# Splitting the probabilities and v of layer 0 into hi and lo parts, with two v tiles in flight

## The chip, the cores and the metric

The kernel runs on one core of one Trainium2 chip. The metric is the device time of one execution in microseconds (us), taken several times; the median counts. One of the executions is recorded by the hardware profiler, and all trace times below count from the start of that span. TensorE's matmuls are called PE, its weight loads PEld, VectorE DVE, ScalarE ACT, GpSimd POOL and the DMA queue's engine SP.

## What is computed

Two layers of a generator over 512 latent and 256 context tokens, width 1024. Only the mixer of layer 0 matters here: four differential heads and four latent heads, each of which ends in probabilities times v.

```python
def diff_attend(q, k, v, lam, lam_init, out_g):
    s = jnp.einsum('bhiqd,bhikd->bhiqk', q, k) * (DA_DK ** -0.5)
    p = softmax_f32(s)
    a = p[:, :, 0] - lam * p[:, :, 1]
    o = jnp.einsum('bhqk,bhkd->bhqd', a.astype(v.dtype), v)
    return rms_norm(o, out_g) * (1.0 - lam_init)

def mla_attend(qn, qr, kn, kr, v):
    s = (jnp.einsum('bhqd,bhkd->bhqk', qn, kn) + jnp.einsum('bhqd,bkd->bhqk', qr, kr)) * ((MLA_NOPE + MLA_ROPE) ** -0.5)
    p = softmax_f32(s)
    return jnp.einsum('bhqk,bhkd->bhqd', p.astype(v.dtype), v)
```

v is 128 wide in both kinds of head. Latent queries read all 768 keys, context queries only the 256 context keys.

## The kernel before

Almost every product of the kernel is written as three rounded products: each operand is split into a hi part (rounded by a ScalarE copy) and a lo part (VectorE subtracts hi from the value), and hi·hi, hi·lo and lo·hi are summed in PSUM (`mm3`, L204 to L207). Probabilities times v in layer 0 (`values`, L677 to L682) is an exception: one product in 32 bits for each block of 128 keys.

The attention of layer 0 is a list of 48 units, a unit being one token tile of 128 queries of one head: 24 of the differential heads (`unit_da`), then 24 of the latent ones (`unit_mla`). Of a head's six units four read six blocks of keys and two read two, so there are 32·6 + 16·2 = 224 blocks, half of them in either kind of head. A unit has three stages:

- S: scores into the one PSUM tile psS, VectorE's negated maximum of a row (nmax, L648, with an addition at L650), ScalarE's exponential with row sums (e, L653). A differential head does this twice a unit, once for each map (m = 0, 1), and there is only one psS: the second map's scores wait until the first map's exponential has read it. VectorE then combines the two maps (L832).
- T: `transpose_p` (L656 to L667) transposes the blocks, three to a PSUM tile psM, and copies each tile to SBUF as pT; the copies go to ScalarE, ScalarE and VectorE in turn (`copy`, kind "P").
- V: `values`, then a VectorE copy of the result to yt.

`pipeline` (L599) puts the stages in the order "S0 T1 f V2 g" in the first half and "S0 T1 V2 f g" in the second: scores of unit i, transposes of unit i-1, values of unit i-2, and at f and g other work from a plan, in half units (`plan0`). The main filler in the differential half is the projection of the next head (`proj_da`, `project`, `proj_tok`): six token tiles, each 24 matmuls into one of two PSUM tiles psW, after which ScalarE copies q and k to qk and the v part to the head's v tile (L766 and L673). The steps of head 2's projection are planned from half unit 9 on, those of head 3 from 21 on. Other filler: the modulation (L323, L331), and in the latent half the output projection (L205 to L207 into psW).

Below this the framework's scheduler orders each engine's instructions by their dependences, so the order on an engine isn't that of the text. A tile that is allocated again is written only once the readers of its earlier use are done. The v tiles come from one ring with `self.vbufs = 3`, the pT tiles from one with two, psM has four tiles in this stage.

Of the kernel before, what the change touches and what calls it, by code (L numbers as in the profile page):

```python
# [10 lines left out]
F32 = mybir.dt.float32  # L11
# [7 lines left out]
P = 128  # L19
# [80 lines left out]
class Kernel:  # L100
# [27 lines left out]
    def psum(self, name, **bufs):  # L128
        """a PSUM pool: M transposes, W projections, O values, S scores (two banks) or T scores (one bank or two)."""
        cm, self.pm = self.pool(name, space=PSUM)  # L130
        self.pbuf = bufs
        return cm
# [20 lines left out]
    def rsqrt_quake(self, ms, n):  # L153
        """1/sqrt by VectorE alone: an integer guess and three Newton steps."""
# [11 lines left out]
    def rsqrt_small(self, ms, n):  # L166
        """1/sqrt by ScalarE's logarithm and exponential and one Newton step."""
        v = self.nc.vector
        y = self.small(n, f"rsy{n}")
        t = self.small(n, f"rst{n}")  # L170
        self.nc.scalar.activation(t, ms, AF.Ln)
        self.nc.scalar.activation(y, t, AF.Exp, scale=-0.5)
        v.tensor_mul(t, y, y)
        v.scalar_tensor_tensor(t, t, -0.5, ms, ALU.mult, ALU.mult)
        v.scalar_tensor_tensor(y, t, 1.5, y, ALU.add, ALU.mult)
        return y
# [21 lines left out]
    def by_k(w, wid):  # L198
        """weights of some k tiles, wid columns each, as a list by k tile."""
        return [tuple(t[:, i * wid:(i + 1) * wid] for t in pair) for pair in w for i in range(2)]  # L200

    def mm3(self, out, w, x, first, last):
        """out += w^T x with w = (hi, lo) stationary and x = (hi, lo) moving."""
# [11 lines left out]
    def constants(self):  # L215
# [13 lines left out]
        # conditions padded to 32 columns, and the columns that sum the four column groups  # L229
# [10 lines left out]
    def lambda_scalars(self):  # L240
# [14 lines left out]
        # power of two not above max(|lam|, 1); its inverse scales the attention rows exactly  # L255
# [9 lines left out]
        # eps carried through the exact scaling  # L265
# [54 lines left out]
    def mod_mm(self, ps, w, k, n):  # L320
        """k tile's part of n columns, in its column group of the array."""
# [3 lines left out]
    def mod_out(self, layer, row, cols, n):  # L325
        """sums over the column groups, transposed to the feature-major table, plus the bias."""
# [12 lines left out]
    def mod_load(self, u):  # L339
        """the columns of shift and scale of two k tiles of layer 0's mixer."""  # L340
# [6 lines left out]
    def mod_pe(self, w, u):  # L347
        """those columns by TensorE, both conditions, in steps: products, table."""
# [17 lines left out]
    def mod_fill(self, layer, cols):  # L366
        """128 columns of the modulation by TensorE, in steps: load, products, table."""
# [13 lines left out]
    def mod_mac(self, layer, cols, conds):  # L381
        """512 columns by VectorE, in steps: a k tile's products each, then the sums over the partitions."""
# [21 lines left out]
    def mod_scale(self, layer, which, ks=slice(0, KD)):  # L404
        """gain * (1 + scale) for both conditions; which = 0 mixer, 1 channel mixer."""
# [10 lines left out]
    def norm_half(self, layer, which, half, acc, dst, pattern, order=range(KD), tile=None, done=None):  # L416
        """h = rmsnorm(x) * a + shift of one half of the tokens into dst's tiles (hi, lo); a step per feature tile.
        pattern: who makes lo; b: VectorE from the unshifted value, v: VectorE, p: GpSimd.
        tile: where h goes unsplit; done: hook of a feature tile."""
# [9 lines left out]
        # the tokens' factors on the partitions, then a column for each token  # L429
# [38 lines left out]
    def wino_h(self, layer, halves, accs, new, keep, pattern):  # L468
        """the channel mixer's input for the products of blocks (features in halves, tokens in halves):
        B = (11 12; 21 22), T1 = 12 - 11, T2 = 22 - T1, T3 = 22 - 12, T4 = 21 - T2, as (hi, lo) by feature tile;  # L470
        the generators of both halves' normalisation."""
# [27 lines left out]
    def new_h(self, hs, n):  # L499
        """dst for norm_half: new (hi, lo) tiles, kept in hs."""  # L500
# [8 lines left out]
    def start(self):  # L509
# [10 lines left out]
        def norm_x(i0):  # L520
            """three token tiles: rms norm without its gain, transposed."""
# [76 lines left out]
    def pipeline(self, units, fill, order):  # L598
        """stages of the units in the order of a step: S scores, T transposes, V values, each so many units behind;  # L599
        f and g: other work."""  # L600
# [9 lines left out]
    def steps(gen, n):  # L610
        """advance a generator by n steps."""
# [15 lines left out]
    def stack(self, s1, s2, pt, m, gain=None):  # L627
        """64 rows of pt (from 64*m) as a stack of hi and lo; s2, if any, is the stack the other way round."""
# [8 lines left out]
    def softmax_rows(self, s, nk, sm, shift=None, scale=None):  # L637
        """exp(scale s - max) and its row sums; s is a score tile in PSUM."""
# [17 lines left out]
    def transpose_p(self, e, nk):  # L656
        """transposes of the probabilities' blocks."""
        nc = self.nc
        pt_ = self.mx.tile([P, 768], F32, tag="pT", name=self.nm("pT"), bufs=self.pbufs)
        for b0 in range(0, nk, 3):  # L660
# [4 lines left out]
            self.copy("P", pt_[:, b0 * P:(b0 + cnt) * P], pt[:, :cnt * P])  # L665
        return pt_

    def copy(self, kind, dst, src):
        """a copy by ScalarE or VectorE, in turns of the kind's pattern."""
# [7 lines left out]
    def values(self, pp, nk, vt, kt0, dst):  # L677
        """probabilities (keys on the partitions) times v in float32, token-major."""
        po = self.psO()[:, :P]
        for b in range(nk):  # L680
            self.nc.tensor.matmul(po, pp[:, b * P:(b + 1) * P], vt[:, kt0 + b], start=b == 0, stop=b == nk - 1)
        self.copy("O", dst, po)  # L682

    def y_split(self, yt, n, dst, gain=None):
        """token-major head outputs, transposed and split into (hi, lo), n token tiles at a time."""
# [14 lines left out]
    def proj_tok(self, ps, w, tt, n, c0=0):  # L700
        """token-major projection of token tile tt: ps[tok, n]; w lists the k tiles' weights."""
# [12 lines left out]
    def norm64(self, x, hf):  # L714
        """rms norm of the 64-wide heads of three token tiles of x."""
# [11 lines left out]
    def k_stacks(self, ks, x, hf, gain=None):  # L727
        """k^T of two 64-wide heads as stacks of hi and lo, for three token tiles."""
# [10 lines left out]
    def q_group(self, x, g):  # L739
        """q^T of a group's two token tiles: for either map its stacks [hi; lo] and [lo; hi]."""  # L740
# [12 lines left out]
    def project(self, w, x, vt, prep, put_v, c0=lambda tt: 0, early=()):  # L753
        """q, k into x and v (hi | lo) of one head, or two, token tile by token tile; then prep(half)'s steps."""
# [20 lines left out]

    def proj_da(self, w, hd, early=()):
        """one head: normalised and roped q and k, k^T stacks, v (hi | lo)."""
# [3 lines left out]
        vt = hd["v"] = mx.tile([P, 6, P], F32, tag="v", name=self.nm("vt"), bufs=self.vbufs)  # L781
# [22 lines left out]
        yield from self.project(w, x, vt, prep, lambda dst, src: self.copy("V", dst, src), early=early)  # L804

    def unit_da(self, hd, g, j):
        """one token tile of queries of a differential head."""
# [32 lines left out]
    def finish_da(self, hd):  # L840
        """rms norm of a head's outputs, token-major; the probabilities' common factor goes in here."""
# [17 lines left out]
    CSEG = ((0, 256), (256, 384), (384, 448))  # L859

    def proj_c(self, w, raws, st):
        """cq, ckv, kr for all tokens; steps of half a token tile."""
# [12 lines left out]
    def prep_c(self, raws, st):  # L875
        """norms, rope of kr, transposes and splits, three token tiles at a time."""
# [43 lines left out]
    def proj_uq(self, pair, hds):  # L920
        """q of two heads, not normalised (the rows' factors go into the softmax), its last part roped."""
# [1015 lines left out]
```

## Time and profile before

| | |
|---|---|
| time of three executions | 1806.55, 1810.14, 1811.74 us |
| median | 1810.14 us |
| span of the profiled execution | 1805.6 us (no own time is given beside it) |
| PE, PEld busy over the span | 94%, 88% |
| DVE, ACT, POOL busy | 79%, 51%, 28% |
| differential units, about 100 to 270 us | PE busy 169.6 of 170 us, DVE 138.3 |
| latent units, about 300 to 435 us | PE busy 130.8 of 135 us, DVE 81.1 |

The busy time of an engine is the union of its instructions. A matmul's duration in the trace contains its latency, and neighbours overlap: 0.28 us long matmuls can start 0.11 us apart. So what a matmul costs the engine is read from the distances between starts in a run of them, for matmuls and for weight loads, and not from durations.

### The profile page before, as it was taken

How to read it: one execution, taken by the hardware profiler on the slowest of the kernel's cores; microseconds unless marked ns; L12 is line 12 of the kernel's file. 1: busy time of each engine (PE TensorE's matmuls, PEld its weight loads, DVE VectorE, ACT ScalarE, POOL GpSimd, SP SyncE). 2: the span in 40 equal slices, each digit the busy share in tenths (PEclk: the TensorE clock that was granted, in tenths of full speed). 3: DMA queues.
4: the chain of work that ended last, by engine and by line, in shares of the span. 5: the costliest groups of instructions: out<-in, count | busy, mean ns of one | idle time of the engine just before them, and what ended most of it. 6: DMA issues, size and time to landing. Idle time of an engine off the chain costs nothing. (4 is left out here: it accounts for less than half of the span.)

```text
span 1805.6 us, 30912 instructions
## 1 busy us (share of the span) xinstructions
PE 1698.4 (94%) x11032; PEld 1593.5 (88%) x11032; DVE 1422.5 (79%) x3060; ACT 926.0 (51%) x2222; POOL 510.2 (28%) x586
## 2 busy tenths in 40 slices
PE   6899999999797999999999989999999879999999
PEld 5789888999677899999989988999998869999997
DVE  4788877566886888888888677888788789888886
ACT  5566667655552233333323466777676555444442
POOL 1300002212664434444434242222221342111110
PEclk9999999999988999999999989999999989999999
DMA  9233233234015434334334313111113423333332
GB/s 315 76 114 114 81 102 96 70 106 165 26 42 182 139 104 137 116 113 128 107 114 147 94 47 97 56 48 53 48 62 111 145 64 105 102 108 102 104 102 82
DMA packets 125754, 186.21 MB, mean 103 GB/s; under 512 B 10625, under 2 KB 63504, under 8 KB 125600
## 3 DMA queue, kind: packets, MB, share of 16 engines
q1 hardware_dynamic: 119360, 172.53, 31.0%
q0 software_dynamic: 2496, 8.49, 1.4%
q10 hardware_dynamic: 3744, 3.23, 0.5%
q8 instruction: 87, 1.43, 0.3%
q14 instruction: 67, 0.55, 0.1%
HBM read 174.70 MB, written 13.70 MB: 104 GB/s over the span
## 5 line engine op out<-in xcount | busy, mean ns | idle before, releaser
L192 ACT CAST wh<-wr 128x512 fp32r<-128x512 f32 (+4 forms) x465 | 287.7, 624 | 382.3 <-PE psM L206 229.0
L194 DVE TENSOR_TENSOR wl<-wr,wh 128x512 fp32r<-128x512 f32 (+3 forms) x433 | 354.6, 823 | 50.1 <-ACT wh L192 43.7
L207 PE MATMUL psD<-zh,wl 128*128 128x384 f32 (+1 forms) x512 | 185.0, 361 | 22.0 <-DVE wl L194 22.0
L205 PE MATMUL psD<-zh,wh 128*128 128x384 f32 (+1 forms) x512 | 183.9, 359 | 6.1 <-ACT wh L192 4.3
L710 PE MATMUL psW<-wh,hh 128*128 128x384 f32 (+2 forms) x543 | 183.4, 339 | 3.9 <-ACT wh L192 3.2
L206 PE MATMUL psD<-zl,wh 128*128 128x384 f32 (+1 forms) x512 | 183.1, 358 | 0.0
L711 PE MATMUL psW<-wl,hh 128*128 128x384 f32 (+2 forms) x543 | 181.7, 335 | 0.4 <-DVE wl L194 0.4
L712 PE MATMUL psW<-wh,hl 128*128 128x384 f32 (+2 forms) x543 | 180.3, 333 | 0.0
L206 PE MATMUL psM<-bl,wh 128*128 128x256 f32 x616 | 175.3, 285 | 4.0 <-POOL bl L466 3.6
L205 PE MATMUL psM<-bh,wh 128*128 128x256 f32 x616 | 174.3, 284 | 5.1 <-ACT bh L465 2.8
L207 PE MATMUL psM<-bh,wl 128*128 128x256 f32 x616 | 173.2, 282 | 0.0
L194 POOL TENSOR_TENSOR wl<-wr,wh 128x512 fp32r<-128x512 f32 (+2 forms) x32 | 39.7, 1245 | 362.8 <-ACT wh L192 344.3
L206 PE MATMUL psM<-hl,wh 128*128 128x384 f32 (+1 forms) x416 | 138.8, 334 | 3.3 <-POOL hl L466 2.9
L205 PE MATMUL psM<-hh,wh 128*128 128x384 f32 (+1 forms) x416 | 139.4, 336 | 1.8 <-ACT hh L465 1.0
L207 PE MATMUL psM<-hh,wl 128*128 128x384 f32 (+1 forms) x416 | 137.6, 331 | 0.0
L1142 POOL TENSOR_TENSOR wr<-wr,wr 128x512 f32<-128x512 f32 x44 | 61.3, 1393 | 267.4 <-DVE wl L194 222.9
L393 DVE SCALAR_TENSOR_TENSOR wr<-wr,silc,wr 128x512 f32<-128x512 f32 x112 | 102.5, 924 | 36.9 <-DMA wr<-in_mod_w 36.8
L207 PEld LDWEIGHTS psD<-zh,wl 128*128 128x128 f32 x512 | 96.5, 189 | 36.1 <-DVE wl L194 28.5
L206 PEld LDWEIGHTS psM<-bl,wh 128*128 128x128 f32 x616 | 118.5, 192 | 8.9 <-POOL bl L466 6.4
L205 PEld LDWEIGHTS psM<-bh,wh 128*128 128x128 f32 x616 | 118.2, 192 | 8.3 <-ACT bh L465 4.1
L1368 POOL TENSOR_TENSOR nbm<-nb,namask 128x128 f32<-128x128 f32 x144 | 64.4, 466 | 200.7 <-DVE nam L1396 183.2
L207 PEld LDWEIGHTS psM<-bh,wl 128*128 128x128 f32 x616 | 118.5, 192 | 0.0
(414 smaller groups left out, 4792.7 us busy)
## 6 DMA issues: line engine op xcount, KB each, us to landing
wr<-in_w_in SPq DMA_DIRECT2D x176, 256.0 KB, 2.9
wr<-in_mod_w SPq DMA_DIRECT2D x96, 256.0 KB, 2.8
mraw<-in_mod_w SPq DMA_DIRECT2D x32, 512.0 KB, 4.0
wr<-in_w_dn SPq DMA_DIRECT2D x50, 256.0 KB, 2.7
wr<-in_w_na SPq DMA_DIRECT2D x28, 384.0 KB, 3.3
wr<-in_w_out SPq DMA_DIRECT2D x36, 256.0 KB, 2.8
wr<-in_w_dn SPq DMA_DIRECT2D x48, 192.0 KB, 2.4
modw<-in_mod_w SPq DMA_DIRECT2D x8, 1024.0 KB, 9.4
```

The source lines that it names most:

```text
L192: nc.scalar.copy(hi[:, :n], raw[:, :n])
L194: (nc.gpsimd if on_pool else nc.vector).tensor_sub(lo[:, :n], raw[:, :n], f32(hi[:, :n]))
L205: t.matmul(out, w[0], x[0], start=first, stop=False)
L206: t.matmul(out, w[0], x[1], start=False, stop=False)
L207: t.matmul(out, w[1], x[0], start=False, stop=last)
L393: v.scalar_tensor_tensor(acc[cd], raw, self.sc[:, k, cd:cd + 1], acc[cd], ALU.mult, ALU.add)
L710: nc.tensor.matmul(ps, hh[:, ts], hi[:, o:o + n], start=k == 0, stop=False)
L711: nc.tensor.matmul(ps, hh[:, ts], lo[:, o:o + n], start=False, stop=False)
L712: nc.tensor.matmul(ps, hl[:, ts], hi[:, o:o + n], start=False, stop=k == KD - 1)
L1142: self.by(fa[2]).tensor_sub(a11, a21, a11)
L1368: nc.gpsimd.tensor_tensor(o, bj[:, t0 + t], m, ALU.add)
```

## The change

Probabilities and v are now kept as hi and lo parts, and each block is three products by `mm3`: stationary pTh with moving v hi, pTh with v lo, pTl with v hi. `transpose_p` writes two tiles, pTh by a ScalarE copy and pTl by a VectorE subtraction, for every group of three blocks, instead of one copy. The v part of a projected token tile goes to the v tile twice in the same way (`put_v`); the v tile is twice as wide and there are two of them instead of three. Nothing else changes but comments; lines move down by up to seven.

```diff
     def transpose_p(self, e, nk):
-        pt_ = self.mx.tile([P, 768], F32, tag="pT", name=self.nm("pT"), bufs=self.pbufs)
+        ph, pl = (self.mx.tile([P, 768], F32R, tag=t, name=self.nm(t), bufs=self.pbufs) for t in ("pTh", "pTl"))
...
-            self.copy("P", pt_[:, b0 * P:(b0 + cnt) * P], pt[:, :cnt * P])
-        return pt_
+            sl = slice(b0 * P, (b0 + cnt) * P)
+            self.put_hi(ph[:, sl], pt[:, :cnt * P], None)
+            self.put_lo(pl[:, sl], pt[:, :cnt * P], ph[:, sl], None)
+        return ph, pl
...
     def values(self, pp, nk, vt, kt0, dst):
         for b in range(nk):
-            self.nc.tensor.matmul(po, pp[:, b * P:(b + 1) * P], vt[:, kt0 + b], start=b == 0, stop=b == nk - 1)
+            w = [t[:, b * P:(b + 1) * P] for t in pp]
+            self.mm3(po, w, [vt[:, kt0 + b, i] for i in range(2)], b == 0, b == nk - 1)
...
+    def put_v(self, hi, lo, src):
+        self.put_hi(hi, src, None)
+        self.put_lo(lo, src, hi, None)
...
     (proj_da)
-        vt = hd["v"] = mx.tile([P, 6, P], F32, tag="v", name=self.nm("vt"), bufs=self.vbufs)
+        vt = hd["v"] = mx.tile([P, 6, 2, P], F32R, tag="v", name=self.nm("vt"), bufs=self.vbufs)
...
-        yield from self.project(w, x, vt, prep, lambda dst, src: self.copy("V", dst, src), early=early)
+        yield from self.project(w, x, vt, prep, lambda dst, src: self.put_v(dst[:, 0], dst[:, 1], src), early=early)
...
     (proj_ukv)
-        vt = mx.tile([P, 6, P], F32, tag="v", name=self.nm("vt"), bufs=self.vbufs)
+        vt = mx.tile([P, 6, 2, P], F32R, tag="v", name=self.nm("vt"), bufs=self.vbufs)
...
-            self.copy("V", vt[:, sl], pv[:, :, 1])
+            self.put_v(vt[:, sl, 0], vt[:, sl, 1], pv[:, :, 1])
...
     (run, layer 0)
-        self.vbufs = 3
+        self.vbufs = 2
```

What this does to the order of instructions is shown at three places.

**Place 1.** On PE, the values of the first unit of head 0, before: vt_679 is head 0's v, the six 32-bit products are one row.

```order
L664 MATMUL psM_1024<-ident,e_917 128x128 x3
L664 MATMUL psM_1029<-ident,e_917 128x128 x3
L331 MATMUL psM_1067<-sel,mrow_995 128x2
L323 MATMUL psM_1070<-mraw_909,silc 32x128 x8
L681 MATMUL psM_1083<-vt_679,pT_948 128x128 x6
L823 MATMUL psS_1010<-kst_681,qs_934 128x384
```

And the same values in the changed kernel, the first nine of 18 rows.

```order
L205 MATMUL psM_1100<-vt_679,pTh_957 128x128
L206 MATMUL psM_1100<-vt_679,pTh_957 128x128
L207 MATMUL psM_1100<-vt_679,pTl_958 128x128
L205 MATMUL psM_1100<-vt_679,pTh_957 128x128
L206 MATMUL psM_1100<-vt_679,pTh_957 128x128
L207 MATMUL psM_1100<-vt_679,pTl_958 128x128
L205 MATMUL psM_1100<-vt_679,pTh_957 128x128
L206 MATMUL psM_1100<-vt_679,pTh_957 128x128
L207 MATMUL psM_1100<-vt_679,pTl_958 128x128
```

Six products became eighteen in one unbroken run, each 128 columns wide.

**Place 2.** On PE, around the scores of head 1's first unit (kst_787 is head 1's k for m = 0), before: psW_1472 is the third token tile of head 2's projection.

```order
L823 MATMUL psS_1444<-kst_787,qs_1193 128x384
L824 MATMUL psS_1444<-kst_787,qs_1194 128x384
L664 MATMUL psM_1468<-ident,e_1340 128x128 x2
L711 MATMUL psW_1472<-wl_1267,hh_370 128x384
L712 MATMUL psW_1472<-wh_1266,hl_371 128x384
L323 MATMUL psM_1485<-mraw_1334,silc 32x128 x3
L823 MATMUL psS_1444<-kst_787,qs_1193 128x384
L824 MATMUL psS_1444<-kst_787,qs_1194 128x384
L323 MATMUL psM_1485<-mraw_1334,silc 32x128 x5
L681 MATMUL psM_1498<-vt_679,pT_1356 128x128 x2
L710 MATMUL psW_1472<-wh_1272,hh_436 128x384
L711 MATMUL psW_1472<-wl_1273,hh_436 128x384
```

In the changed kernel the same scores (kst_793, psS_1520) stand right behind the end of head 2's second token tile (psW_1488).

```order
L715 MATMUL psW_1488<-wh_1326,hl_508 128x384
L331 MATMUL psM_1516<-sel,mrow_1456 128x2
L830 MATMUL psS_1520<-kst_793,qs_1238 128x384
L831 MATMUL psS_1520<-kst_793,qs_1239 128x384
L830 MATMUL psS_1520<-kst_793,qs_1238 128x384
L831 MATMUL psS_1520<-kst_793,qs_1239 128x384
L664 MATMUL psM_1545<-ident,e_1400 128x128 x2
L323 MATMUL psM_1563<-mraw_1394,silc 32x128 x8
L205 MATMUL psM_1576<-vt_679,pTh_1416 128x128
L206 MATMUL psM_1576<-vt_679,pTh_1416 128x128
L207 MATMUL psM_1576<-vt_679,pTl_1417 128x128
L205 MATMUL psM_1576<-vt_679,pTh_1416 128x128
```

The next projection row comes 40 rows below that of psW_1488, behind the scores of three more maps (psS_1530, psS_1616, psS_1626) and the last values of head 0 (psM_1710).

```order
L830 MATMUL psS_1626<-kst_794,qs_1238 128x384
L831 MATMUL psS_1626<-kst_794,qs_1239 128x384
L830 MATMUL psS_1626<-kst_794,qs_1238 128x384
L831 MATMUL psS_1626<-kst_794,qs_1239 128x384
L205 MATMUL psM_1710<-vt_679,pTh_1543 128x128
L206 MATMUL psM_1710<-vt_679,pTh_1543 128x128
L207 MATMUL psM_1710<-vt_679,pTl_1544 128x128
L323 MATMUL psM_1746<-mraw_1574,silc 32x128 x8
L713 MATMUL psW_1550<-wh_1308,hh_290 128x384
L714 MATMUL psW_1550<-wl_1309,hh_290 128x384
```

Four maps' scores now stand in a row without a projection's product between them; before, every one had such products behind it. At head 3's projection (psW of its third tile) the order has the same shape, with the scores of four maps ahead of it.

**Place 3.** On ACT at the same point: in the changed kernel the first copies into head 2's v tile (vt_1367).

```order
L617 CAST pTh_1652<-psM_1654 128x384
L617 CAST pTh_1652<-psM_1660 128x384
L617 CAST qs_1639<-psM_1635 64x256
L653 ACTIVATE e_1621,s_86_665<-psS_1616,nmax_1622 128x768
L617 CAST vt_1367<-psW_1370 128x128
L617 CAST vt_1367<-psW_1488 128x128
L653 ACTIVATE e_1631,sume_293_1615<-psS_1626,nmax_1632 128x768
```

Before, a corresponding stretch had the v copy of a later tile right behind that tile's copy of q and k.

```order
L617 CAST qs_1555<-psM_1552 64x256
L653 ACTIVATE e_1538,s_86_665<-psS_1533,nmax_1539 128x768
L617 CAST qs_1556<-psM_1552 64x256
L766 COPY qk_1306<-psW_1580 128x256
L673 COPY vt_1307<-psW_1580 128x128
```

The copies of both tiles (psW_1370, psW_1488) moved to behind the third of the four exponentials, and both psW tiles are held until then.

## Rows read from the trace of the kernel before

**Rows 1.** The page: the span.

```profile
span 1805.6 us, 30912 instructions
```

**Rows 2.** Windows: stretch, length, busy PE, PEld, DVE, ACT, POOL (instructions), PEclk, DMA, GB/s.

```profile
100.00:270.00 170.00, 169.60 (x1368) 152.81 (x1368) 138.27 (x352) 108.31 (x327) 2.66 (x3) 1.00 0.37 107
...
300.00:435.00 135.00, 130.84 (x926) 125.95 (x925) 81.08 (x203) 79.36 (x237) 21.97 (x27) 1.00 0.29 93
```

**Rows 3.** PE by line and form: count | busy us, mean ns | idle before.

```profile
L681 PE MATMUL psM<-vt,pT 128*128 128x128 f32 x448 | 61.6, 281 | 0.1
L323 PE MATMUL psM<-mraw,silc 128*32 128x128 f32 x512 | 21.5, 283 | 0.0
```

**Rows 4.** Timeline, PEld around 317 us: start, length, what.

```profile
317.10 1.42 PEld L681 LDWEIGHTS psM<-vt,pT 128*128 128x128 f32 x12
318.44 0.25 PEld L689 LDWEIGHTS psM<-ident,yt 128*128 128x128 f32 x2
```

**Rows 5.** Timeline, PE at 1193 us: layer 1's rounded products, two of 128 columns.

```profile
1193.07 0.28 PE L1444 MATMUL psM<-pl,vt 128*128 128x256 f32 x1
1193.19 0.22 PE L1444 MATMUL psM<-ph,vt 128*128 128x128 f32 x1
1193.25 0.27 PE L1444 MATMUL psM<-pl,vt 128*128 128x128 f32 x1
1193.36 0.34 PE L1444 MATMUL psM<-ph,vt 128*128 128x256 f32 x1
```

**Rows 6.** Timeline, PEld at the same point.

```profile
1193.19 0.19 PEld L1444 LDWEIGHTS psM<-pl,vt 128*128 128x128 f32 x1
1193.30 0.19 PEld L1444 LDWEIGHTS psM<-ph,vt 128*128 128x128 f32 x1
1193.41 0.19 PEld L1444 LDWEIGHTS psM<-pl,vt 128*128 128x128 f32 x1
```

**Rows 7.** L681 and L1444: weight loads, ns min/median/max.

```profile
L681 PEld LDWEIGHTS psM<-vt,pT x448: 186/192/338, 106.2 to 432.3; 128*128 128x128 f32 x150
L1444 PEld LDWEIGHTS psM<-pl,vt x160: 187/192/333, 1112.5 to 1406.9; 128*128 128x128 f32 x160
```

**Rows 8.** DVE and ACT by form, 95 to 440 us.

```profile
L675 DVE COPY pT<-psM 128x384 f32<-128x384 f32 x21 | 11.6, 552 | 0.4 <-PE psM L664 0.3
L623 DVE TENSOR_TENSOR yl<-psM,yh 128x384 fp32r<-128x384 f32 x8 | 4.1, 552 | 0.8 <-ACT yh L617 0.8
L623 DVE TENSOR_TENSOR qs<-psM,qs 64x256 fp32r<-64x256 f32 x64 | 26.8, 418 | 4.5 <-ACT qs L617 3.1
L675 DVE COPY yt<-psM 128x128 f32<-128x128 f32 x48 | 13.8, 287 | 9.4 <-PE psM L681 9.1
L648 DVE TENSOR_REDUCE nmax<-psS 128x1 f32<-128x768 f32 x46 | 43.9, 955 | 28.5 <-PE psS L1038 15.3 <-PE psS L824 12.8
L653 ACT ACTIVATE e<-psS,nmax 128x768 f32<-128x768 f32 x31 | 28.0, 903 | 16.7 <-DVE nmax L648 10.1 <-DVE nmax L650 6.6
L673 ACT COPY pT<-psM 128x384 f32<-128x384 f32 x43 | 19.6, 481 | 12.9 <-PE psM L664 12.6
```

**Rows 9.** Timeline: one map of 256 keys, from its scores to the next.

```profile
125.19 0.38 PE L823 MATMUL psS<-kst,qs 128*128 128x256 f32 x1
125.74 0.42 DVE L648 TENSOR_REDUCE nmax<-psS 128x1 f32<-128x256 f32 x1 [0.16 <-PE psS L824]
126.20 0.16 DVE L650 TENSOR_TENSOR nmax<-nmax,lnf 128x1 f32<-128x1 f32 x1
126.39 0.48 ACT L653 ACTIVATE e<-psS,nmax 128x256 f32<-128x256 f32 x1 [0.64 <-DVE nmax L650]
127.14 0.37 PE L823 MATMUL psS<-kst,qs 128*128 128x256 f32 x1
```

**Rows 10.** Timeline: matmuls of 384 columns in a run.

```profile
300.97 0.34 PE L1038 MATMUL psS<-krT,qs 128*128 128x384 f32 x1
301.84 0.34 PE L1038 MATMUL psS<-krT,qs 128*128 128x384 f32 x1
```

## The prediction

> **What bounds the kernel now.** I read the windows of the two kinds of unit first, then PE by line and form, then single runs of matmuls in the timeline, and last the vector engines. The change lies wholly in the attention of layer 0, about 100 to 435 us of a span of 1805.6 us [rows 1]. In the differential units PE is busy 169.6 of 170 us and in the latent ones 130.8 of 135 [rows 2]: whatever is added to PE there has next to no idle time to hide in, while DVE has 32 of 170 and 54 of 135 us idle. So the stage's limit is PE, and the question is what a product costs PE.
>
> Values are 448 matmul records for 224 blocks, two to a 32-bit product [rows 3]. A run of twelve weight loads (six blocks) begins at 317.10 us and the next load follows at 318.44: 1.34/12 = 0.112 us a record, 0.223 us a block [rows 4]. The 50.0 us that 448 of them take is what the change replaces.
>
> **What three rounded products cost.** Before the change no rounded product of 128 columns stands in this stage, but layer 1 has pairs of them. The matmuls start at 1193.07 (256 columns), 1193.19 (128), 1193.25 (128) and 1193.36 (256) [rows 5]. The second short one starts only 0.06 us behind the first, which looks like a quarter of a 32-bit product; but the next start takes 0.11 again. The weight loads show why: they start at 1193.19, 1193.30 and 1193.41, 0.11 us apart, however short the matmul [rows 6]. A load takes 192 ns at the median for rounded operands and for 32-bit ones alike [rows 7], and one overlaps its neighbour only so far. So in a run each product of 128 columns costs the 0.11 us of its weight load, as each record of the 32-bit product does. Three products with a weight load each take 672 x 0.1115 = 74.9 us in place of 448 x 0.1115 = 50.0: **plus 25.0 us**, half of it in either kind of unit. The lower bound is the 0.06 us step: 672 x 0.06 = 40.3, a gain of 9.7 us; the upper is 0.12, the step behind 256 columns (1193.07 to 1193.19, [rows 5]): 80.6, a loss of 30.6. I take 0.1115, because the values now stand in runs of 18 with nothing longer between them.
>
> The Trainium skill speaks against this choice on one point. TensorE: Matmul & The Clock Gate, "Back-to-back issue gap", gives a warm isolated gap of N/2.4 + 2.5 ns, 56 ns for 128 columns, and 81 ns for a sustained stream of load and matmul; by these, as estimates, the values would take 37.6 or 54.4 us, a gain of 12.4 or a loss of 4.4. The same page, "Weight-path perf modes", has a fast weight load for operands that are not 32-bit floats; the equal load times of [rows 7] show none of it for these rounded operands. The trace decides for 0.11.
>
> **Two v tiles.** Head 2's v goes where head 0's was, so its first copy must wait for head 0's last values, which come in the step of head 1's second unit. Its projection is planned from two steps earlier on. Two token tiles of it fill the two psW tiles, and the third can't start. In the order, four maps' scores (psS_1520 to psS_1626) then follow each other on PE with no projection product between them, where before each had some behind it. There the chain through the single psS sets the pace: scores, maximum, exponential, next scores. An undisturbed turn for 256 keys took 127.14 - 125.19 = 1.95 us [rows 9]. For 768 keys the scores are four matmuls of 0.174 us (five steps in 301.84 - 300.97, [rows 10]) instead of two of 256 columns at 0.12 [rows 5], plus 0.46; the maximum takes 955 instead of 420 ns, plus 0.53, and the exponential 903 instead of 480, plus 0.42 [rows 8, 9]. That is 3.36 us with the addition of L650 (m = 0) and 3.2 without (m = 1). From the first of these scores to the fourth: 3.36 + 3.2 + 3.36 = 9.9 us; with the fourth's own 0.70, three values and eight products of the modulation (0.042 us each, 21.5/512, [rows 3]) the next projection product starts 11.2 us after the first scores. PE's work in between: 16 score matmuls 2.8, ten transposes and twelve values at 0.11 together 2.4, 24 products of the modulation 1.0, a few short sums 0.3: 6.5 us. **About 4.5 us of PE stand idle**, and the same once more for head 3 (four maps, nearly the same filler, v of head 1 free only then): **plus 9 us together**. Bounds: nothing, if the turns run faster than one that I call undisturbed or other work fills them; 16 us, if ACT and DVE, which carry the chain and the new splits in one queue each, make the turns half as long again. For the latent heads the earlier reader is done by the time of the first copy (at least in the plan), so I price that at nothing, as I do the wider v tile itself.
>
> Queued behind the waiting copy on ACT is the fourth exponential, whose scores come later anyway, so the wait blocks nothing that was ready. What was filler there isn't lost: it comes behind, in a stretch where PE is full, but it no longer covers the chain.
>
> **The splits.** 64 groups of 384 columns and 16 of 256 get a subtraction on DVE (552 and 418 ns for such operands, [rows 8]): 42.0 us. DVE loses 21 copies of 552 ns and five of 256 columns, which I price like the subtraction of 418: 13.7 us. The lo part of v adds 24 subtractions of 128x128 (nearest: the copy of 287 ns) and twelve of 128x256 (418): 11.9 us. **DVE plus 40 us**, about 19 in either kind of unit and the rest (head 0's v) ahead of them. ACT takes over 26 copies of at most 481 ns: plus 12 us. In the differential units DVE rises from 138.3 to about 158 of then 170 + 12.5 + 9 = 191 us, 83%; in the latent ones from 81 to about 100 of 147. Neither becomes the bound, and PE's longer runs of values cover them, so I take nothing for it; were the existing idle time of DVE in the differential units fixed (waits for scores, 28.5 us before nmax over the whole stage, [rows 8]), its 19 us would stretch that half by 7 more than PE's 12.5 do. pTl also comes one subtraction (0.55 us) later than pT did, and psM is held that much longer; values stand a whole step behind their transposes (7 us a unit), which covers both.
>
> **Sum.** 25.0 + 9 = 34 us on a span of 1805.6, 1839.6. The median of the runs shown is 4.5 us above that span, and I leave this distance as it is: **1844 us**. PE's few idle microseconds of today (0.4 and 4.2 in the two windows, [rows 2]) could swallow some of the 25, by at most as much.
>
> **Rivals.**
> - The wait is hidden. Then only the products count: 1810 + 25 = 1835. For it: the scheduler moved the blocked copies out of other work's way. Against it: the order shows four maps without filler.
> - The vector side stretches the chain: the splits delay nmax and the exponential in all 24 differential units, and the two stalls are longer. 25 + 16 + 7, and a few more in the latent half: 1860. For it: DVE already 81% busy in that half, the chain's turns of 6.6 us for two maps close to the 7.1 us (170/24) that a unit takes. Against: a unit gains 0.5 us of values to hide in.
> - It gets faster. The mechanism is a product paid by its columns and not by its load: the step of 0.06 us between the two short products holds for a whole run. Then the values fall by 9.7 us, and with the wait hidden the time is 1800. It decides below 50.0/672 = 0.074 us a product. Against it stand the load distances of [rows 6].
> - In between, at some 0.08 us a product and with the stalls small, the change is lost in the measurement: near 1812. The Trainium skill's 81 ns would be such a case; no run here shows it.
>
> **How the numbers follow.** Chances: the forecast 0.62, the hidden wait 0.14, the vector side 0.15, faster 0.05, no visible change 0.04. The forecast's own range is 1836 to 1853. Over all cases, 1828 to 1863 leaves out the two last cases, some 1 in 10, and the far tail of the vector side. About 0.3% is what a measurement of this kernel tells from no change. Slower by more: 0.91; within: 0.04; faster: 0.05.
>
> **What would show it.** In the changed kernel's trace: 672 records on the values' lines with weight loads 0.11 us apart in runs of 18 (0.06 would make the first step wrong). PE idle, by some 4 us each, behind the scores of head 1's and head 2's first units, released by the exponential, and a first projection matmul right after head 0's and head 1's last values. The differential stage longer by 21 us, the latent one by 12, later stages shifted without growing. DVE some 40 us busier in all. The prediction is wrong if PE shows idle time at every unit's scores (the vector side), if the load distances shrink, or if a later stage gives time back.

## The result and the profile after

The changed kernel takes **1879.4 us** (median of four executions, 1877.4 to 1880.9) where the kernel before took 1810.9 beside it: the ratio is 1.037, with a 95% interval of 1.036 to 1.039. It is slower, as forecast, but by 68.5 us and not by 34; the range given ended at 1863.

The page of the changed kernel begins with its span (before: [rows 1]).

```profile
span 1878.9 us, 31488 instructions
```

Windows of both halves, cut in each kernel at its own first differential score, its first latent score and 8 us behind its last one; the columns are those of [rows 2]. The changed kernel:

```profile
82.00:346.00 264.00, 242.23 (x1826) 215.80 (x1824) 196.02 (x497) 149.56 (x456) 13.34 (x20) 0.94 0.28 80
346.00:503.00 157.00, 148.29 (x1064) 142.59 (x1057) 99.63 (x243) 86.32 (x255) 23.07 (x29) 0.99 0.23 71
```

The kernel before, cut in the same way:

```profile
81.00:300.00 219.00, 214.69 (x1727) 192.89 (x1726) 179.28 (x453) 143.42 (x448) 13.78 (x21) 0.99 0.34 99
300.00:437.00 137.00, 132.84 (x937) 127.95 (x936) 82.10 (x205) 79.94 (x239) 21.97 (x27) 1.00 0.28 91
```

The differential half is 45 us longer, the latent half 20, what stands behind them 7 and what stands ahead 1 (between these two executions there are 73 us, 5 more than between the medians). In the differential half PE stands idle for 21.8 us (264 - 242.23) where it was 4.3; its granted clock is 0.94 in the mean, after 0.99. At only two levels, 1.2 and 2.4 GHz, a mean of 0.94 over 264 us is some 32 us at the lower one (2 x 0.06 x 264; the trace's clock record has 34.1), which loses at most half of that; before it was 3.4 us, by the same record. So of the 45 us, 12 are more products, 17.5 more idle time, and up to 15 a slower clock. The forecast had 12.5, 9 and nothing. In the latent half idle time grew from 4.2 to 8.7 us, which with 12.5 us of products and up to 2 of clock makes 19 of its 20 us. DVE is no busier in relation: 74% of the half in place of 82%.

The products themselves, PE by line and form (columns as [rows 3]):

```profile
L205 PE MATMUL psM<-vt,pTh 128*128 128x128 f32 x224 | 63.3, 283 | 0.6 <-DVE pTl L623 0.6
L206 PE MATMUL psM<-vt,pTh 128*128 128x128 f32 x224 | 62.1, 277 | 0.0
L207 PE MATMUL psM<-vt,pTl 128*128 128x128 f32 x224 | 61.9, 276 | 0.0
```

and a run of them in the timeline of the weight loads, against [rows 4, 6]:

```profile
330.42 0.19 PEld L207 LDWEIGHTS psM<-vt,pTl 128*128 128x128 f32 x1
330.54 0.19 PEld L205 LDWEIGHTS psM<-vt,pTh 128*128 128x128 f32 x1
330.65 0.19 PEld L206 LDWEIGHTS psM<-vt,pTh 128*128 128x128 f32 x1
330.76 0.19 PEld L207 LDWEIGHTS psM<-vt,pTl 128*128 128x128 f32 x1
...
332.10 0.19 PEld L207 LDWEIGHTS psM<-vt,pTl 128*128 128x128 f32 x1
```

The 16 loads from 330.42 to 332.10 are 0.112 us apart, as forecast. The splits are there too, DVE and ACT by form (against [rows 8]):

```profile
L648 DVE TENSOR_REDUCE nmax<-psS 128x1 f32<-128x768 f32 x48 | 45.8, 955 | 31.0 <-PE psS L831 17.3 <-PE psS L1045 13.2
L623 DVE TENSOR_TENSOR pTl<-psM,pTh 128x384 fp32r<-128x384 f32 x64 | 34.3, 550 | 1.9 <-ACT pTh L617 1.5
L617 ACT CAST pTh<-psM 128x384 fp32r<-128x384 f32 x64 | 28.6, 481 | 17.4 <-PE psM L664 17.2
```

nmax waits for the scores of 768 keys hardly longer than before (31.0 us, before 28.5). What PE waits for is told by the list of waits, 80 to 510 us (us in total, times, longest):

```profile
PE psS L830 <- ACT e L653: 9.0, 11, 2.1
PE psM L664 <- DVE e L839: 2.8, 4, 1.0
PE psS L1041 <- ACT e L653: 2.4, 3, 1.5
PE psM L1002 <- DVE pTl L623: 2.1, 2, 1.9
```

The score chain leads. One of its stalls, in the timeline of the changed kernel, PE with the two vector engines that carry the chain, and PE 5 us later:

```profile
206.22 0.44 PE L830 MATMUL psS<-kst,qs 128*128 128x384 f32 x1 [0.30 <-ACT e L653]
...
207.22 0.96 DVE L648 TENSOR_REDUCE nmax<-psS 128x1 f32<-128x768 f32 x1 [0.35 <-PE psS L831]
...
208.22 0.90 ACT L653 ACTIVATE e<-psS,nmax 128x768 f32<-128x768 f32 x1 [0.95 <-DVE nmax L648]
...
209.26 0.44 PE L830 MATMUL psS<-kst,qs 128*128 128x384 f32 x1 [2.08 <-ACT e L653]
...
211.22 1.54 PE L664 MATMUL psM<-ident,e 128*128 128x128 f32 x6 [0.98 <-DVE e L839]
...
215.26 0.52 PE L831 MATMUL psS<-kst,qs 128*128 128x384 f32 x1
215.58 0.52 PE L830 MATMUL psS<-kst,qs 128*128 128x384 f32 x1
215.90 0.52 PE L831 MATMUL psS<-kst,qs 128*128 128x384 f32 x1
```

From one map's scores to the next it is 3.04 us, and PE stands idle in 2.08 of them. Later matmuls of 384 columns start 0.32 us apart where [rows 10] had 0.174. The windows of this stretch show the clock (columns as above):

```profile
200.00:206.80 6.80, 6.50 (x74) 5.74 (x73) 2.58 (x9) 2.82 (x9) 0.00 (x0) 1.00 0.34 89
206.80:210.80 4.00, 1.36 (x7) 0.72 (x5) 2.81 (x7) 2.09 (x5) 0.00 (x0) 0.99 0.42 117
210.80:221.00 10.20, 9.78 (x60) 8.60 (x61) 6.25 (x17) 4.69 (x16) 0.00 (x0) 0.50 0.35 102
221.00:228.00 7.00, 7.00 (x42) 7.00 (x41) 4.40 (x13) 2.25 (x8) 0.00 (x0) 1.00 0.02 4
```

Behind 4 us in which PE was busy for 1.36 the clock stands at the lower level for 10.2 us, in which PE is 96% busy. The two stalls that the forecast named run from the first of four maps' scores to the next projection product, 137.3 to 151.9 and 202.8 to 217.8 us:

```profile
137.30:151.90 14.60, 11.45 (x93) 8.95 (x91) 9.91 (x24) 7.74 (x21) 0.00 (x0) 0.79 0.26 74
202.80:217.80 15.00, 11.64 (x97) 9.32 (x93) 9.23 (x22) 6.98 (x20) 0.00 (x0) 0.77 0.39 107
```

### The profile page after: what moved, and what is told of

Read it like the earlier page. It is cut to its first block, busy times and chain, and to the rows that moved or that the text cites. A ratio compares the mean times of both kernels' runs of the same rounds, so it can differ in the third digit from the quotient of the medians.

```text
span 1878.9 us, 31488 instructions
## 1 busy us (share of the span) xinstructions
PE 1745.4 (93%) x11256; PEld 1635.8 (87%) x11256; DVE 1459.4 (78%) x3150; ACT 938.3 (50%) x2248; POOL 511.5 (27%) x586
## 6 DMA issues: line engine op xcount, KB each, us to landing
modw<-in_mod_w SPq DMA_DIRECT2D x8, 1024.0 KB, 10.2
```

## The experiments

The theories at the start: **1** (the forecast's own, with a fall of the clock added to it: 0.11 us a product, and two v tiles that stall the chain), **2** (the splits stretch the chain), **3** (the short rounded products bring the clock down by themselves). "Theory 4" is in the first text a cheaper product; from the second group on it is that the order of the instructions is at fault.

**Parts alone.** The products without splits and ring (e1):

```diff
-            self.nc.tensor.matmul(po, pp[:, b * P:(b + 1) * P], vt[:, kt0 + b], start=b == 0, stop=b == nk - 1)
+            w = pp[:, b * P:(b + 1) * P]
+            x = vt[:, kt0 + b]
+            self.mm3(po, (w, w), (x, x), b == 0, b == nk - 1)
```

> The kernel before with its three v tiles and its copies as they were; pT and v are written as rounded tiles, and each block is three rounded products of the same pT and v (the lo parts are left out: hi times hi three times). Only the number of products on PE changes. Theory 1 (0.11 us a product, and the rest of the loss comes from the ring of two v tiles, whose stalls also let the granted clock fall): the values cost 672 x 0.1115 - 50.0 = 25 us, the granted clock in the differential half stays near before's (3 us at 0.5): 1836 us, give or take 4. Theory 2 (the splits on DVE and ACT stretch the chain of a unit): the same 1836 here. Theory 3 (the short rounded products themselves bring the clock down): stretches at 0.5 appear here too, some 30 us of them, and the time is 1850 or more. Theory 4 (short products in a run cost less than 0.11): under 1822.

The ring without products and splits (e2: `self.vbufs = 2` in the kernel before):

> The kernel before, with two v tiles in place of three and nothing else changed. Theory 1 (the ring stalls the score chain at head 2's and head 3's first units, and the clock falls behind the idle time): plus 9 us for the two stalls and up to some 10 more for the clock, 1820 to 1830 us, with stretches at a granted clock of 0.5 behind the stalls. Theory 2 (the splits): the ring costs little by itself, 1811 to 1818. Theory 3 (the short products): the same 1811 to 1818, and no more time at a clock of 0.5 than before.

The splits of the probabilities alone (e3):

```diff
+            self.put_hi(ph[:, sl], pt[:, :cnt * P], None)
+            self.put_lo(pl[:, sl], pt[:, :cnt * P], ph[:, sl], None)
...
+            self.nc.tensor.matmul(po, f32(pp[b % 2])[:, b * P:(b + 1) * P], vt[:, kt0 + b], start=b == 0, stop=b == nk - 1)
```

> The kernel before, with three v tiles, with the changed kernel's split of the transposed probabilities (a ScalarE copy to pTh and a VectorE subtraction to pTl for each psM tile); each block is still one 32-bit product, of pTh or pTl in turn, with the unsplit v (half of the sum's terms are left out, so the output isn't the attention's). It adds what the splits ask of ACT and DVE and of psM, without more products. Theory 1: DVE gains about 28 us and ACT about 10, hidden behind PE: 1811 to 1814 us, clock as before. Theory 2 (splits stretch the chain): 1825 or more, with PE idle at each unit's scores, released by the exponential or nmax. Theory 3 (the short products): 1811.

Two products a block instead of three, in the changed kernel (e4):

```diff
+            t.matmul(po[:, :256], w[0], vt[:, kt0 + b].rearrange("p x d -> p (x d)"), start=b == 0, stop=False)
+            t.matmul(po[:, :P], w[1], vt[:, kt0 + b, 0], start=False, stop=b == nk - 1)
+        self.nc.vector.reduce_sum(dst, po[:, :256].rearrange("p (x d) -> p d x", x=2), axis=AX.X)
```

> The changed kernel, with its splits and its two v tiles; hi of the probabilities times v hi and v lo side by side is one product of 256 columns into two halves of the PSUM tile, lo times v hi is one of 128 columns, and VectorE's sum of both halves takes the place of the copy to yt. A block then has two weight loads in place of three. If the load sets the price at 0.11 us (and 0.12 for 256 columns), a block costs 0.23 us in place of 0.335: 224 x 0.105 = 24 us less than the changed kernel's 1879.4, so 1856 us, and what is left above before (45 us) is not the products' own. Theory 3 (short products lower the clock): more than 24 us come back, 1840 or less, since the run of short products is gone. Theories 1 and 2 (ring and clock, or splits): 1852 to 1860, with the same idle time and the same stretches at a clock of 0.5.

Measured against 1812.9 us of before: e1 1870.4 (1.0315, 1.029 to 1.035), e2 1830.1 (1.010, 1.007 to 1.013), e3 1820.9 (1.004, 1.003 to 1.006), e4 1856.3 (23 us under the changed kernel). e4 came as expected: a weight load less in each block gives its price back. e2, 17 us longer, lies where theory 1 put it, e3 between theories 1 and 2. e1 was a surprise: 57 us for products alone, where all theories but the third had 25 or less. Its loads are 0.11 us apart as well (18 of them from 328.06 to 329.95). But its PE is idle for 18 us in the differential half:

```profile
81.00:335.00 254.00, 235.90 (x1826) 211.12 (x1825) 179.57 (x453) 144.28 (x446) 12.71 (x21) 0.96 0.29 83
```

The order of the instructions had moved with the products. Counted in PE's order: how many projection products stand between a map's scores and the next map's, for the first 36 of the 48 differential maps.

```
before 47 14 15 13  4 11  6  7 11 5 9  0 14  8 16  9 15 24 21 8 9 2 10 10 12 12 11 25 13 11 31  9 9 3 5  3
e1     47 14 15 13  4  0  4  0  9 0 2 24 12 12 16  8 12 36 15 0 3 6  6 30 12 12 13 23 18  6 17  4 1 0 2 36
after  45 14 17 13 12  2  3  0 16 0 0 10  0  0  0 48 14 34 14 2 9 0  6 17  0  0  0 72 13 11 22 12 3 0 0 23
```

Over all maps one has none in the kernel before, six in e1, eight in e2 and 13 in the changed kernel; e3 has two. What is missing there stands in heaps elsewhere (48, 72). With 18 products in the values the scheduler puts the projection elsewhere, ring or no ring: the changed kernel with three v tiles (e8, below) has seven such maps, the very seven of the changed kernel that lie outside its two rows of four maps. Those two rows, with the other six, come with the ring: e2 has two such rows as well, of five maps each, and e8 has none.

**Order against products.** A table ties PE's matmuls of layer 0's attention into the order of another kernel (e5, e6, e7):

```diff
+    def in_order(self):
+        mm = [i for i in self.nc.cur_bb.bb.instructions if i.engine == mybir.EngineType.PE and "Matmul" in type(i).__name__]
+        seq = [mm[a + j] for a, n in PE_ORDER for j in range(n)]
+        for a, b in zip(seq, seq[1:]):
+            self.tc.add_manual_dep(b, a.name, mybir.DependencyInfo(mybir.DependencyClass.NoSync, mybir.DependencyReason.DATA), reason="order")
```

> The kernel e1_products_only (three rounded products of the same pT and v, lo parts left out, three v tiles), with PE's matmuls of layer 0's attention tied into the order in which they stand in the kernel before, each 32-bit product replaced in its place by its three products. e1 was 57 us longer than before where 25 were expected, and its order on PE has lost the projection's products that stood behind scores. Theory 4 (the scheduler moved the projection away from the scores, PE then waits for maximum and exponential, and the clock falls behind the waits): only the products' own 25 us are left, 1838 us give or take 5, with some 4 us at a granted clock of 0.5 in the differential half as before. Theory 3 (short rounded products in runs cost more than their loads, or bring the clock down by themselves): as e1, 1865 to 1872.

> The kernel before, with its 32-bit products and nothing else changed but the order on PE: layer 0's attention is tied into the order of e1_products_only, one product where that has three. Theory 4 (order): the loss of e1 without its products, 32 us and rather more, since six products between two scores cover less than eighteen: 1840 to 1855 us, with stretches at a clock of 0.5 of 15 us and more in the differential half. Theory 3 (short products): 1811 to 1818.

e8 is the changed kernel with three v tiles, e7 adds before's order on PE:

```diff
-                raws.append(self.mx.tile([P, 3, 512], F32, tag="craw" if tt == 0 else "qk", name=self.nm("craw"), bufs=1 if tt == 0 else 2))
+                raws.append(self.mx.tile([P, 3, 512], F32, tag="v" if tt == 0 else "qk", name=self.nm("craw"), bufs=3 if tt == 0 else 2))
...
-        self.vbufs = 2
+        self.vbufs = 3
```

> The changed kernel with three v tiles; the third takes the place of the first raw tile of the latent projection, which uses a slot of the same ring. Theory 1 (ring of two): the 17 us that the ring of two cost by itself come back, 1862 us. Theory 4 (order): the ring's stalls and the moved projection are the same loss and don't add up; 1866 to 1880, with e1's idle time behind the scores.

> The same, the changed kernel with three v tiles, and PE's matmuls of layer 0's attention tied into the order of the kernel before. Everything that the change does is in it (splits, three products, the wider v tile) but the order and the ring of two. Theory 4 (order): products 25 and splits 8, 1846 us give or take 5. Theory 2 (splits): the splits' late pTl and their time on DVE make scores and transposes wait in this order as well, 1855 or more.

Measured, before at 1811.2: e6 1851.2 (1.021, 1.018 to 1.025). **e1's order on PE alone, with the 32-bit products, costs 40 us** (ACT and DVE follow as the scheduler puts them). Its windows show idle PE, 24 us, and its waits the score chain:

```profile
81.00:325.00 244.00, 219.89 (x1718) 194.82 (x1717) 179.78 (x454) 145.00 (x448) 13.72 (x21) 0.98 0.30 89
```

```profile
PE psS L823 <- ACT e L653: 7.6, 8, 2.2
PE psM L664 <- DVE e L832: 4.9, 6, 2.2
```

e5 1847.6 (1.019, 1.017 to 1.022): 23 us of e1's 57 gone, but 36 left, not 25. e8 1879.4: the third v tile gives back nothing. The two rows of four are gone, and PE waits for the exponential at L830 for 3.6 us in place of 9.0; but the time at the lower clock grew in its place (see the end). e7 1864.3 (1.028, 1.025 to 1.031): 15 less by PE's order, and 17 more than e5.

**All orders kept.** e5's order on ACT and DVE was still made anew. e10 ties these two as well, with one more table each; what is left to differ from before is three products for one.

> As e5_products_old_order (three rounded products of the same pT and v, lo parts left out, three v tiles), but besides PE's matmuls also ACT's and DVE's instructions of layer 0's attention are tied into the order of the kernel before: it differs from before in nothing but the three products for one. e5 left 36 us where the products' own are 25, with a stall of 2.7 us at 281 us that an ACT copy ended and the clock at 0.5 behind it. Theory 4 (order, of the other engines too): 1836 us give or take 4, the stall gone. If 36 us are the products' own price (waits that longer values cause in any order): 1847 as e5.

1832.1 us (1.012, 1.010 to 1.014): **plus 21**. With that theory 3 is out as the main cause: the same short products are all in it, and 36 of e1's 57 us are gone. PE's idle time is 1.9 us less than before in the two halves, its busy time 23.9 us more:

```profile
80.00:313.00 233.00, 228.92 (x1835) 208.65 (x1834) 179.18 (x452) 143.75 (x447) 13.83 (x21) 0.97 0.32 94
313.00:458.00 145.00, 142.47 (x1047) 139.63 (x1046) 82.47 (x204) 80.22 (x237) 21.33 (x27) 1.00 0.26 85
```

The clock has a part in that as well: from 299.8 to 313.5 us it stands at the lower level, with PE busy throughout, which loses up to 7 us where before lost 2. So the products by themselves come to 19 to 24 us here.

Two more with tables: e12 is e7 with e4's products, e9 the changed kernel in PE's order of e2.

> The kernel of e7_three_v_old_order (splits, three v tiles, PE's order of before), with the products of e4_wide_products: hi times v hi and v lo as one product of 256 columns, lo times v hi as one of 128, and VectorE's sum of the two halves. By the load distances a block costs 0.23 us as before's two records do, so only the splits are left. If costs add up: e7's 1864 less 24, 1840 us. If e7's 17 us over e5 come from splits and longer values together (theory 4: order and lengths that no longer fit each other), more is given back, 1820 to 1830, near the 8 us of e3_splits_only.

> The changed kernel itself, ring of two and all, with PE's matmuls of layer 0's attention tied into the order of e2_ring_of_two (the 32-bit kernel that was scheduled with two v tiles; 1830 us), each product replaced in its place by its three. Theory 4 (the order that came with the three products costs some 15 us over a better one, as e8 against e7 and e1 against e5): 1860 to 1868 us. Theory 1 (the ring itself is the loss, in any order): 1875 or more.

e12 took 1842.2 (22 less than e7: costs add up). e9 took 1881.6: no gain, a miss. That order also has eight maps without a projection product, in the two rows that the ring makes.

e13 asks the same of the whole change: three v tiles, and all three engines in before's order but for what writes pTh, pTl and v. e14 is that with e4's products; DVE's order is free in it.

> The changed kernel with three v tiles (as e8), with PE's, ACT's and DVE's instructions of layer 0's attention tied into the order of the kernel before, but for the copies and subtractions that write pTh, pTl and v, which the scheduler still places. All of the change's work is in it. If the loss is order alone (theory 4): e10's 1832 and what the splits cost in e3, 8 at most: 1832 to 1842 us, with few stalls and the clock near 0.974. If the splits' work itself makes PE wait (theory 2): 1850 or more, like e7's 1864, with waits for pTl, for the exponential behind pTh on ACT and for nmax behind pTl on DVE.

> The same with the products of e4_wide_products (one of 256 columns and one of 128 in place of three; VectorE's sum of both halves in place of the copy to yt), PE's and ACT's orders kept; DVE's is left to the scheduler, since its instructions aren't the same. Theory 4: 21 us less than e13, near the kernel before, 1815 to 1825 us. Theory 2: e12's 1842 or a little less.

e13 took 1844.0 (1.018, 1.016 to 1.021): **the change with three v tiles and the old orders costs 32 us (28 to 38 by the interval): 21 as in e10, and some 11 more, which are the splits' by difference.** Its profiled execution is the longest (span 1850.4, mean clock 0.966; the other three have 0.969 to 0.973). What the splits make PE wait for stands in its waits, 80 to 480 us:

```profile
PE psM L1002 <- DVE pTl L623: 2.6, 2, 2.3
PE psM L917 <- DVE pTl L623: 1.8, 1, 1.8
PE psS L830 <- ACT e L653: 1.3, 2, 0.9
```

L1002 transposes kn of a latent head, L917 the latent projection, both into a psM tile that the late subtraction still reads. e14 took 1842.7, some 20 more than expected: its PE is idle 26 us in both halves together, so what the cheaper products left free seems to have gone into waits, 4.4 us of them at the same kn transposes for pTl. Which part of it DVE's free order has, and which the sum that replaces the copy, was not taken apart. It also takes no less time than e12 (1842.2), in which ACT's order is free: what a kept order is worth depends on what else is in the kernel.

**Waits and clock.** e15 fills eight of the waits in the changed kernel, with PE's order tied to the changed kernel's own:

```diff
+            for _ in range(FILL.get(self.nmap, 0)):
+                nc.tensor.transpose(sc[:, 1, 384:512], self.ident, self.ident)
```

> The changed kernel in its own order (PE's tied to it), with twelve transposes of the identity added behind the scores of eight maps, those that have no projection product and at most one block group's values behind them before the next scores: 96 more products of 0.11 us, into columns of psS that nobody reads. They lie where PE waits for the exponential, the chain itself is unchanged. If the clock falls because of these waits: the stretches at 0.5 near 146 us (6.8 us) and 211 us (10.2 us) go, the time at 0.5 in the differential half falls from 33 us to some 16, and the time by half of what goes, less what the 10.6 us of products lengthen elsewhere: 1868 to 1876 us. If the clock falls for another reason: the stretches stay, 1879 us or up to 8 more.

1889.5 us (1.0425, 1.041 to 1.044), 10 more than the changed kernel. It isn't the clean test that was meant: nmax waited for the fillers, as DVE's timeline shows, so the chain got longer by them (scores at 141.60 and 145.96 us, 4.36 apart; in the changed kernel the same two are 3.06 apart).

```profile
143.92 0.96 DVE L648 TENSOR_REDUCE nmax<-psS 128x1 f32<-128x768 f32 x1 [2.77 <-PE psS L834]
```

The clock did answer: the stretches at 146 (6.8 us) and 211 us (10.2 us) are gone, one of 3.4 at 151 is there, and the mean of the half rose to 0.97. Though six of the eight chains are 1.3 to 1.4 us longer each, the half took 267 us, 3 more.

```profile
82.00:349.00 267.00, 244.69 (x1920) 219.40 (x1919) 195.51 (x496) 149.90 (x457) 13.36 (x21) 0.97 0.27 79
```

So in these two places the idle time brings the clock down; that is as far as this run shows it. The other 9 us between the two profiled executions were lost behind the half.

## Why the prediction was right in direction and half the size

- **The price of a product was right.** 0.112 us between loads in the changed kernel; 25 us by the sum, and 19 to 24 for the products, 21 us in all, when nothing else differs (e10). The prediction's allowance for old idle time explains 1.9 us of the gap. The Trainium skill's 81 ns for a sustained stream of load and matmul (TensorE: Matmul & The Clock Gate, "Back-to-back issue gap") is not what these products show, nor its 56; e4 confirms the load as the price from the other side.
- **The step that failed is "Two v tiles".** It looked at the order where the ring had changed it, found four maps in a row without a projection product, twice, and priced them at 9 us of idle time; for the rest of the order it had no price. The two stalls were there, much as worked out (the two windows above): their first two turns took 3.42 and 3.06 us, 3.44 and 3.04 (3.36 and 3.2 worked out), though the third, in which the clock fell, took 5.0 and 5.6. PE is idle 3.2 and 3.4 us in them, not 4.5 each. So some 11 of the 17.5 us more idle time in this half stand elsewhere, behind the seven other uncovered maps and other waits of the list above. Nor does the time hang on the ring: with three tiles (e8) the two stalls are gone and the time is the same, since the scheduler lays the projection elsewhere as soon as the values are 18 products (e1, e8: six and seven uncovered maps without any ring of two). e1's order costs 40 us without a single product more (e6). Of the 68 us, 15 go away with PE's old order (e8 less e7) and 20 with that of ACT and DVE (e7 less e13).
- **"The splits ... so I take nothing for it" failed by some 8 to 11 us** (e3, e13). DVE rose by 34 us in the two halves (16.7 and 17.5), close to the 38 worked out, and didn't become the bound. The argument that values stand a whole step behind covers values; it doesn't cover who takes the psM tile next, the transposes of L1002 and L917 in e13, of L1002 and L692 in the changed kernel (2.1 and 1.4 us of waiting for pTl).
- **The clock had no term.** Up to 15 of the 45 us in the differential half come from time at 1.2 GHz, half of them in and right behind the two stalls (17 of the 34.1 us at that level). Idle time was priced by its length alone.
- **"Later stages shifted without growing"** missed 7 us: in the windows of the rest PE takes 4.6 us more busy time for the same matmuls (1294.0 after 1289.3) and is idle 2.4 us longer. By the trace's clock record 88.7 us of it are at the lower level, after 78.5, and those 10 us are enough for the busy time. Why the clock fell there more often is open; and since the two profiled executions differ by 5 us more than the medians, part of the 7 may be spread between executions.
- The rival "the vector side stretches the chain" came nearest with 1860, but by another cause: nmax's waits grew by 4.6 us in all (31.0 and 5.7 for maps of 768 and 256 keys, after 28.5 and 3.6), and DVE did not become the bound. The two cheap-product rivals are excluded by the product's price, the hidden wait by PE's idle time behind the scores.

What stays open is why the scheduler moves the projection, as no trace shows its reasons, and how the 35 us of order split between waiting and clock, since the two come together. Which of ACT and DVE has how much of the 20 is open as well.

## What to carry to other kernels

When a change alters how many instructions a block has, the scheduler may lay other work anew far from the edit; count over the whole stage how much filler stands behind each link of a chain, before and after, not only at the place that the edit points to. Price a wait on TensorE with what its clock takes behind it. To part a change's own cost from that of its order, tie the new kernel's engines to the old order: here that took 35 of 68 us away.

## What was not expected of the hardware

Behind a short wait the clock can stay low for many times the wait's length. In e8 PE is busy 6.0 of 7.8 us, with one wait of 1.8 us before the scores at 246.7, and the clock then stands at 0.5 for 17.1 us in which PE never rests; the same happens at 486.7, behind a wait of 1.1 us:

```profile
240.00:247.80 7.80, 6.02 (x58) 5.42 (x56) 6.38 (x17) 4.72 (x19) 0.00 (x0) 1.00 0.24 67
247.80:264.90 17.10, 17.10 (x93) 15.66 (x93) 5.25 (x18) 3.40 (x12) 0.00 (x0) 0.50 0.22 62
264.90:280.00 15.10, 14.91 (x118) 12.73 (x117) 8.36 (x23) 8.07 (x30) 0.00 (x0) 1.00 0.24 70
```

That is how e8, with 4.5 us less idle time than the changed kernel in the differential half, ends at the same time: its mean clock is 0.93 in that half and 0.95 in the latent one, where the changed kernel has 0.94 and 0.99. Not every short wait is followed by a lower clock, and no rule is worked out here that tells them apart. In e6 the clock stays up behind one of 2.2 us that ends at 122.4:

```profile
118.80:122.40 3.60, 1.47 (x21) 0.99 (x21) 3.32 (x9) 2.39 (x9) 0.00 (x0) 1.00 0.41 122
122.40:125.80 3.40, 3.11 (x21) 2.91 (x22) 2.29 (x7) 2.26 (x6) 0.00 (x0) 1.00 0.11 32
125.80:140.00 14.20, 13.98 (x115) 12.87 (x114) 6.66 (x21) 5.52 (x17) 0.00 (x0) 1.00 0.27 76
```

In e10 two waits of 0.9 and 1.0 us stand ahead of the 13.7 us at the lower level:

```profile
296.40:299.80 3.40, 1.50 (x12) 0.98 (x15) 3.17 (x7) 2.73 (x11) 2.76 (x4) 1.00 0.09 26
299.80:313.50 13.70, 13.70 (x96) 11.89 (x97) 6.62 (x18) 5.33 (x21) 5.50 (x11) 0.50 0.40 119
```

The Trainium skill (TensorE: Matmul & The Clock Gate, "HAM oscillation — how this bites in real kernels") tells of a kernel whose waits for DMA, of 3 to 5 us, bring the clock down. The rows of this case agree that idle time does (200 to 228 us above, e15), but here the waits are of 1 to 2 us; what the rows add is the 17 us at the lower level with the engine busy throughout.
